# A hybrid attention/mLSTM encoder layer: the first stage loads x first, takes the modulation weights and the first projection by halves in an order written out by hand, and TensorE keeps the written order with its transposes among the products

## The chip, the cores and the metric

The kernel runs on one core of one Trainium2 chip. Its engines are TensorE (PE in the profile; its weight loads are PEld), VectorE (DVE), ScalarE (ACT), GpSimd (POOL) and SyncE (SP), which issues most of the DMAs. Each engine works through its own queue in order. The metric is the device time of one execution in microseconds (us), as the median of several runs; less is better.

## The reference: what is computed

One encoder layer on x of 2048 x 1024 in float32, then a last RMSNorm. Only the head of the layer matters here: the modulation vectors, the first norm, and the columns of the input projection that give the attention's values, the mLSTM's values and the gates.

```python
def hybrid_layer(x, c, w_mod, b_mod, g_norm1, w_in, ...):
    mod = jax.nn.silu(c) @ w_mod + b_mod                 # 6 x 1024
    shift1, scale1, gate1, shift2, scale2, gate2 = [m[:, None, :] for m in jnp.split(mod, N_MOD, axis=-1)]
    hmix = rms_norm(x, g_norm1) * (1.0 + scale1) + shift1
    proj = hmix @ w_in
    q_a, k_a, v_a, q_m, k_m, v_m, o_m, gates = jnp.split(proj, IN_SPLITS, axis=-1)
    ...                                                  # windowed attention, two mLSTM scans, w_out
    hff = rms_norm(x, g_norm2) * (1.0 + scale2) + shift2
    gte, up = jnp.split(hff @ w_ffn_in, 2, axis=-1)
    ff = (jax.nn.silu(gte) * up) @ w_ffn_out
    return x + gate2 * ff
```

## The kernel before

All products are made in three passes of a split float32: each operand is a rounded high part and the rest as a low part, and `mm3` (L55 to L58) issues high x high, high x low and low x high. So every operand needs a split, a copy (ACT or DVE) and a subtraction (DVE or POOL).

The first stage is the block under the pool `sw`. It does these things:

- **Modulation.** A modulation vector m is made by halves z of 512 columns. `load_mod` (L177) brings a half of `w_mod` in four tiles `wmod` of 512 KB. `mod_sum` (L190) sums the eight 128-row pieces, each scaled by a column of silu(c): on DVE into `macc` (L195, L197), or, for the first `n_pe` pieces, on TensorE (L201). TensorE turns the sum into columns (`modps`, L207 or L211), and `mod_bias` (L216) adds the bias. Only m = 1 (scale1) and m = 0 (shift1) are needed before the first norm is complete; m = 2 to 5 are made later, a half at a time, by `mod_row` (L320): four more 512 KB loads (L331), eight DVE operations (L335, L337), the split of `macc` (`macch`, `maccl`, L124 and L125), and two products with ones (`modrow`, L343 and L344).
- **Norm and transpose.** x comes in four blocks n of 512 rows, each four tiles `xt` of 512 KB. `normalised` (L146) squares on ACT (L151), takes the reciprocal root on DVE (`rsqrt`, 12 small operations), and scales the rows (L155 on ACT for block 0, L157 on DVE for the others). Then, for each of eight pieces k, `turned` (L159) makes four transposes on TensorE into one PSUM bank, "b" or "d" in turn, with one buffer each; ACT evicts the bank with scale and shift into `ntmp` (L164, two buffers); DVE splits it into `hT` (L172, L173).
- **Products.** `nat_mm` (L359) makes, for each of 16 tiles tt of 128 rows, 24 products of 272 columns into `pa` and 24 of 384 columns into `pv`. The weights are `wnl`/`wnh`, split from `wnr` in two halves by `split_nat` (L306). For tiles 0 to 2 the first half (k = 0 to 3) comes before the second.
- **Evictions and stores.** For each tile, ACT and DVE write `vs` (L404, L405, one buffer) and `gn` (L406), ACT writes `va` (L407, L408, two buffers), and SP stores `vst_d` (L412) and `vaug_d` (L413). A `mod_row` step follows from tile 4 on (`next(vecs)`, L411).

In this stage a scheduler sets the order of every engine's queue from its own estimates, taking the program's order as priority. From the second stage on, TensorE's order is the program's (`hand`), and shortly after also that of the other engines (`win`). SP's loads run in order too: an issue that waits for a free buffer holds up every issue behind it. Each DMA also waits for the one eight issues earlier.

The pool `s1` holds what only the norm needs; two of the four buffers that `mod_row` uses for m = 3 to 5 lie in its place (the pool `w`, opened after `xs.close()`), so their loads wait for the last transposes of block 3. The stage's end is the last `modrow` and the last tile's products; then the second stage begins with the transposes of the gates.

Of the kernel before, what the change touches and what calls it, by code (L numbers as in the profile page):

```python
# [21 lines left out]
P = 128  # L22
T = 2048
D = 1024
# [12 lines left out]
def hybrid_layer_kernel(  # L37
# [52 lines left out]
    O_C, O_G1, O_G2, O_CB, O_CW, O_BM, O_GA, O_GM = 0, 8, 16, 24, 32, 56, 104, 108  # L90
# [55 lines left out]
    def normalised(pl, xt, on_act=False):  # L146

        ssq = pl.tile([P, 4], F32, tag="ssq", name="ssq")
        for i in range(4):
            jk = pl.tile([P, D], BF16, tag="junk", name="junk", bufs=1)  # L150
            act.activation(jk, xt[i], AF.Square, accum_out=ssq[:, i:i + 1])  # L151
        r = rsqrt(pl, ssq, 4, D, "rs")
        for i in range(4):
            if on_act:
                act.activation(xt[i], xt[i], AF.Copy, scale=r[:, i:i + 1])  # L155
            else:
                dve.tensor_scalar(xt[i], xt[i], r[:, i:i + 1], None, MUL)  # L157
# [8 lines left out]
    def norm_block(pl, xt, gs, shift, dst):  # L166

        normalised(pl, xt, len(hT) == 1)
        for k in range(KT):
            t = pl.tile([P, 512], F32, tag="ntmp", name="ntmp", bufs=2)  # L170
            turned(t, xt, k, "bd"[k % 2], gs, shift)
            dve.tensor_copy(dst(0, k), t)  # L172
            dve.tensor_tensor(dst(1, k), t, dst(0, k).bitcast(F32), SUB)  # L173
            yield True
# [14 lines left out]
    def mod_sum(pl, m, z, ws_, n_pe):  # L189

        acc = pl.tile([P, 512], F32, tag="macc", name="macc")
        for k in range(n_pe, KT):
# [3 lines left out]
            else:  # L196
                dve.scalar_tensor_tensor(acc, w, sc_col[:, k:k + 1], acc, MUL, ADD)  # L197
        if n_pe:
# [9 lines left out]
        else:  # L208
            ps = bank("d", "modps")
            for k in range(4):  # L210
                pe.matmul(ps[:, k:k + 1], acc[:, k * P:(k + 1) * P], ones[:, 0:1], start=True, stop=True)  # L211
        mod_bias(m, z, ps)

# [28 lines left out]
    with tc.tile_pool(name="sw", bufs=2, side="right", reuse_waits="tile") as sw:  # L242
        c8 = s1.tile([8, P], F32, name="c8", bufs=1)
        rows = s1.tile([112, P], F32, name="rows", bufs=1)
        sp.dma_start(c8, c.rearrange("o (a b) -> (o a) b", b=P))
        def load_x(n):
# [8 lines left out]
        wm = {(1, 0): load_mod(1, 0)}  # L255
        xts = [load_x(0)]
        for src, o, n in ((c, O_C, 8), (g_norm1, O_G1, 8), (g_norm2, O_G2, 8), (conv_b, O_CB, 8),
                          (conv_w[0], O_CW, 24), (b_mod, O_BM, 48), (g_attn_out, O_GA, 4), (g_mlstm_out, O_GM, 4)):
            sp.dma_start(rows[o:o + n, :], src.rearrange("o (a b) -> (o a) b", b=P))
# [8 lines left out]
        ps = bank("a", "colps")  # L268
        pe.transpose(ps[:, :112], rows, ident[:112, :112])
        dve.tensor_copy(cols, ps[:, :112])  # L270
        dve.tensor_scalar(cvw, cols[:, O_CW:O_CW + 24].rearrange("p (j k) -> p j k", j=3), 0.5, None, MUL)
        dve.tensor_scalar(cvb, cols[:, O_CB:O_CB + KT], 0.5, None, MUL)
        dve.tensor_scalar(gml, cols[:, O_GM:O_GM + HM], 0.5, None, MUL)
# [6 lines left out]
        sp.dma_start(bg, b_gates[0].partition_broadcast(P))  # L280
# [6 lines left out]
        def start_mod(z):  # L287

            for m in (1, 0):
                if (m, z) not in wm:  # L290
                    wm[m, z] = load_mod(m, z)
            for m, n_pe in ((1, 0), (0, (0, 4)[z])):
                mod_sum(s1, m, z, wm[m, z], n_pe)
# [21 lines left out]
        def norm1(n, xt):  # L315
            hT.append(Kt(n, f"hT{n}"))
            return norm_block(s1, xt, gs1, mod[:, 0, :], hT[n])
# [41 lines left out]
        def nat_mm(n, i, pa, pv, ks):  # L359
            for o, cs in ((pa[:, :NA], slice(0, NA)), (pv[:, :NV], slice(NA, NA + NV))):  # L360
                for k in ks:
                    lh, ll = (hT[n](s, k, slice(i * P, (i + 1) * P)) for s in (0, 1))
                    mm3(o, lh, ll, wh[:, k, cs], wl[:, k, cs], k == 0, k == KT - 1)

        gn = cp.tile([P, 2, 2, HM, NT], F32, name="gn")
        bgv = bg.rearrange("p (d y h) -> p y d h", d=2, y=2)
        start_mod(0)
        wn = [load_nat(z) for z in range(2)]
        split_nat(0, wn[0])
        g0 = norm1(0, xts[0])  # L370
        deque(islice(g0, 4), 0)
        ops = {i: (bank("gga"[i], "pa"), bank("acc"[i], "pv")) for i in range(3)}
        for i in range(3):
            nat_mm(0, i, *ops[i], range(4))
        start_mod(1)
        split_nat(1, wn[1])
        deque(g0, 0)
        xts += [load_x(1), load_x(2)]
        for n in range(NB):
            if n + 1 < NB:  # L380
                deque(norm1(n + 1, xts[n + 1] if n < 2 else load_x(3)), 0)
            if n == 1:
                vecs = mod_row(2)
            if n + 2 == NB:
                deque(vecs, 0)
                wrow = deque(["w1h", "w1l", "wm0", "wm1"])
                xs.close()
                wp = ctx.enter_context(tc.tile_pool(name="w", bufs=1, side="left", reuse_waits="tile"))
                wslots.extend([(wp, 0), (wp, 1)])
                vecs = chain.from_iterable(mod_row(m) for m in range(3, 6))  # L390
            if n + 1 == NB:
                w_first = proj_cols(C_KM)
            for i in range(4):
                tt = 4 * n + i
                if n == 0 and i < 3:
                    pa, pv = ops[i]
                    nat_mm(n, i, pa, pv, range(4, KT))
                else:
                    pa, pv = bank("g", "pa"), bank("a", "pv")
                    nat_mm(n, i, pa, pv, range(KT))  # L400
# [9 lines left out]
                if n:  # L410
# [475 lines left out]
    hand, win = ExitStack(), ExitStack()  # L886
    steps = [gates(), w_out_ops()]
    due = [0, next(steps[1])]
    hand.enter_context(tc.manual_schedule(engines={mybir.EngineType.PE}))
# [931 lines left out]
```

## Time and profile before

| | us |
|---|---|
| median of 3 runs | 2373.31 |
| the runs | 2373.31, 2383.68, 2371.09 |
| the profiled execution's own time | 2375.25 |
| its span | 2373.5 |
| TensorE busy in the span | 2256.7 (95%) |
| TensorE busy from 0 to 50 us, summed from windows of 10 us | 26.0 |
| TensorE's waits for `macch` from 60 to 215 us | 13.7 |
| mean granted TensorE clock | 0.988 |

A row of the timeline gives start, duration, engine, line, operation, output and inputs, form and count, and in brackets the idle time ahead of it with what ended it. A row of windows gives for each engine its busy time and its instructions, then the granted clock, the share of the DMA engines and GB/s. What a wait is worth is read in its stage: an engine's idle time costs only where the next thing on TensorE hangs on it.

### The profile page before, as it was taken

What the parts mean: (1) busy time and instruction counts of PE and PEld (TensorE: products, weight loads), DVE (VectorE), ACT (ScalarE), POOL (GpSimd) and SP (SyncE); (2) the same over time, 40 slices, a digit from 0 to 9 for tenths busy, and PEclk for the clock granted to TensorE, in tenths of its full rate; (3) what the DMA queues carried; (4) which work ended last, traced back from release to release, by engine and by line L of the source; (5) the groups of instructions that cost most, each with busy time, mean ns of one, the idle gap of its engine ahead of it and who ended that gap; (6) DMA issues with size and microseconds to landing.
All of it is one profiled execution on the core that took longest, in us unless ns stands there. A gap on an engine that the chain in (4) does not pass through costs nothing.

```text
span 2373.5 us, 32635 instructions
## 1 busy us (share of the span) xinstructions
PE 2256.7 (95%) x10811; PEld 1870.8 (79%) x10811; DVE 1587.3 (67%) x2998; ACT 1074.2 (45%) x2205; POOL 1029.9 (43%) x876
## 2 busy tenths in 40 slices
PE   5988999999999989898999999999999999999998
PEld 4987777888788867787878878788888888888886
DVE  6777577667687877878555685755655536684684
ACT  4523555545487745435453443543434323233452
POOL 1004643334334434516555555465656545592020
PEclk9999999999999989999999999999999999999999
DMA  7575845577666566863343553533333373443452
GB/s 294 175 217 181 266 147 171 171 219 205 189 178 182 176 200 200 269 241 124 111 168 94 169 164 107 200 107 94 107 93 107 97 242 127 154 152 98 145 196 95
DMA packets 355517, 393.40 MB, mean 166 GB/s; under 512 B 21396, under 2 KB 253196, under 8 KB 355348
## 3 DMA queue, kind: packets, MB, share of 16 engines
q1 hardware_dynamic: 355348, 391.32, 51.9%
q8 instruction: 85, 1.39, 0.2%
q14 instruction: 84, 0.69, 0.1%
HBM read 272.06 MB, written 119.19 MB: 165 GB/s over the span
## 4 chain that ended last, share of the span: by engine, by line
PE 52%; DVE 3%; DMA 1%; issue 1%; ACT 1%; SPq 0%; POOL 0%; DVEq 0%; ACTq 0%; POOLq 0%
PE fp L56 11%; PE fp L57 11%; PE fp L58 11%; PE fo L58 6%; PE fo L57 6%; PE fo L56 6%; DVE S L1363 1%; PE ops L56 1%; PE ops L58 1%; PE ops L57 1%; DVE T L1323 0%; DVE A L1363 0%; PE trn L163 0%; DVE B L1323 0%; DMA hop_d<-n 0%
## 5 line engine op out<-in xcount | busy, mean ns | idle before, releaser
L424 PE MATMUL gps<-hT,whi 128*128 128x512 f32 x1088 | 398.2, 420 | 0.0
L56 PE MATMUL fo<-w,ah 128*128 128x512 f32 x616 | 241.7, 392 | 2.6 <-ACT ah L1605 2.6
L58 PE MATMUL fo<-w,al 128*128 128x512 f32 x616 | 241.8, 393 | 0.5 <-DVE al L1606 0.5
L57 PE MATMUL fo<-w,ah 128*128 128x512 f32 x616 | 241.5, 392 | 0.0
L424 PE MATMUL gps<-hT,wlo 128*128 128x512 f32 x544 | 228.3, 420 | 0.0
L56 PE MATMUL fp<-T,S 128*128 128x512 f32 x528 | 211.0, 400 | 12.2 <-ACT s L1508 6.4
L424 PEld LDWEIGHTS gps<-hT,whi 128*128 128x128 f32 x1088 | 202.6, 191 | 24.3 <-issue 0.2
L57 PE MATMUL fp<-T,S 128*128 128x512 f32 x528 | 209.1, 396 | 0.0
L58 PE MATMUL fp<-T,S 128*128 128x512 f32 x528 | 209.0, 396 | 0.0
L1606 DVE TENSOR_TENSOR al<-al,ah 128x1024 fp32r<-128x1024 f32 x77 | 112.7, 1468 | 130.2 <-ACT ah L1605 130.0
L1363 DVE TENSOR_TENSOR A<-graw,A 128x512 fp32r<-128x512 f32 x86 | 107.6, 1270 | 118.3 <-ACT A L1362 116.4
L1605 ACT ACTIVATE ah<-al 128x1024 fp32r<-128x1024 f32 x77 | 81.6, 1060 | 193.5 <-DMA al<-a_d 190.5
L56 PEld LDWEIGHTS fo<-w,ah 128*128 128x128 f32 x616 | 115.6, 188 | 29.2 <-ACT ah L1605 3.0
L58 PE MATMUL fp<-B,A 128*128 128x512 f32 x352 | 137.6, 391 | 0.0
L56 PE MATMUL fp<-B,A 128*128 128x512 f32 x352 | 137.6, 391 | 0.0
L57 PE MATMUL fp<-B,A 128*128 128x512 f32 x352 | 137.6, 391 | 0.0
L58 PEld LDWEIGHTS fo<-w,al 128*128 128x128 f32 x616 | 115.5, 188 | 27.2 <-DVE al L1606 1.0
L57 PEld LDWEIGHTS fo<-w,ah 128*128 128x128 f32 x616 | 115.5, 188 | 26.3
L56 PEld LDWEIGHTS fp<-T,S 128*128 128x128 f32 x528 | 100.7, 191 | 36.9 <-ACT u L1516 7.9
L716 POOL TENSOR_SCALAR ap<-ap,adn 128x384 f32<-128x384 f32 (+1 forms) x128 | 73.1, 590 | 127.1 <-DVE adn L714 57.4
L58 PEld LDWEIGHTS fp<-T,S 128*128 128x128 f32 x528 | 100.6, 191 | 22.6
L1363 DVE TENSOR_TENSOR S<-sf,S 128x512 fp32r<-128x512 f32 x86 | 87.3, 1017 | 45.8 <-ACT S L1362 45.8
(416 smaller groups left out, 6107.5 us busy)
## 6 DMA issues: line engine op xcount, KB each, us to landing
al<-a_d SPq DMA_DIRECT2D x77, 512.0 KB, 4.1
wmod<-in_w_mod_dram SPq DMA_DIRECT2D x48, 512.0 KB, 6.3
graw<-in_w_ffn_in_dram SPq DMA_DIRECT2D x43, 512.0 KB, 5.0
a_d<-ka SPq DMA_DIRECT2D x66, 256.0 KB, 2.4
bc<-bc_d SPq DMA_DIRECT2D x64, 256.0 KB, 3.8
hop_d<-n SPq DMA_DIRECT2D x56, 256.0 KB, 3.8
a_d<-u SPq DMA_DIRECT2D x55, 256.0 KB, 3.5
mqk<-qk_d SPq DMA_DIRECT2D x48, 256.0 KB, 4.4
```

Source lines behind the costliest of these rows:

```text
L56: pe.matmul(o, lh, rh, start=first, stop=False, skip_group_check=skip)
L57: pe.matmul(o, lh, rl, start=False, stop=False, skip_group_check=skip)
L58: pe.matmul(o, ll, rh, start=False, stop=last, skip_group_check=skip)
L424: pe.matmul(ps, w[i == 2][:, k, :], hT[n](i == 1, k), start=(k == 0 and i == 0), stop=(k == KT - 1 and i == 2))
L716: pool.tensor_scalar(self.p[g][:, :self.NK], self.p[g][:, :self.NK], dn[:, g:g + 1], 0.0, MUL, ADD)
L1363: dve.tensor_tensor(t[:, 1, :], f, t[:, 0, :].bitcast(F32), SUB)
L1605: act.activation(ah, al.bitcast(F32), AF.Copy)
L1606: dve.tensor_tensor(al, al.bitcast(F32), ah.bitcast(F32), SUB)
```

## The change

The first stage is rewritten in eight respects.

1. SP loads x's block 0 first, then scale1's and shift1's first halves, the projection weights' first half, scale1's second half, the weights' second half, shift1's second half, then blocks 1 and 2 of x. Before, scale1's first half came first, then x, nine small loads, and the rest.
2. The small vectors are split into two tiles; the part that is needed first (g_norm1 and b_mod) is issued by ACT, the rest by SP after block 2, and turned in the second block (`columns_of`).
3. Four of the eight pieces of scale1's first half are summed on TensorE instead of DVE; for shift1's second half this was so before.
4. From the start to the transposes of block 0's second half, all engines keep the program's order (`pre`, `hand`). The weights' second half is split after scale1's second sum, not among block 0's first pieces.
5. TensorE keeps the program's order for the whole stage. `nat_mm` yields after each k, and the table EVERY says after how many k a batch of four transposes of the next block is issued: block 1's in tile 3, block 2's two in each of tiles 4 to 7, block 3's all in tile 8. Before, block 1's stood among the second halves of tiles 0 to 3, and block 3's among the first 24 products of tile 8.
6. x's block 3 is loaded in the first round instead of the third.
7. `xs.close()` comes after tile 8's products, and tile 9 takes no `mod_row` step. The first `modrow` of m = 3 comes after tile 10, the last after tile 15.
8. `hand` is entered here instead of in the second stage.

The order of the second stage and of everything behind it is the same on all engines.

```diff
-    def norm_block(pl, xt, gs, shift, dst):
-
-        normalised(pl, xt, len(hT) == 1)
-        for k in range(KT):
-            t = pl.tile([P, 512], F32, tag="ntmp", name="ntmp", bufs=2)
...
+    def turned_split(pl, xt, k, gs, shift, dst):
+
+        t = pl.tile([P, 512], F32, tag="ntmp", name="ntmp", bufs=2)
+        turned(t, xt, k, "bd"[k % 2], gs, shift)
+        dve.tensor_copy(dst(0, k), t)
+        dve.tensor_tensor(dst(1, k), t, dst(0, k).bitcast(F32), SUB)
...
+        hand, pre = ExitStack(), ExitStack()
+        others = {getattr(mybir.EngineType, e) for e in ("DVE", "Activation", "Pool", "SP")}
+        hand.enter_context(tc.manual_schedule(engines={mybir.EngineType.PE}))
+        pre.enter_context(tc.manual_schedule(engines=others))
...
+        for src, o, n in ((g_norm1, O_G1, 8), (b_mod, O_BM, 48)):
+            act.dma_start(rows[0][o:o + n, :], src.rearrange("o (a b) -> (o a) b", b=P))
...
-        wm = {(1, 0): load_mod(1, 0)}
         xts = [load_x(0)]
...
+        wm = {(m, 0): load_mod(m, 0) for m in (1, 0)}
...
+        wn = [load_nat(0)]
+        wm[1, 1] = load_mod(1, 1)
+        wn.append(load_nat(1))
+        wm[0, 1] = load_mod(0, 1)
+        xts += [load_x(1), load_x(2)]
...
+        ms = {(m, z): mod_sum(s1, m, z, wm[m, z], 4 if m == 1 - z else 0) for z in range(2) for m in (1, 0)}
+        ssq = squares(s1, xts[0])
+        r = rsqrt(s1, ssq, 4, D, "rs")
+        next(ms[1, 0])
+        scaled(xts[0], r, True)
+        next(ms[0, 0])
...
+        scales(0)
+        split_nat(0, wn[0])
+        ops = {i: (bank("gga"[i], "pa"), bank("acc"[i], "pv")) for i in range(3)}
+        for k in range(4):
+            turned_split(s1, xts[0], k, gs1, mod[:, 0, :], hT[0])
+        for i in range(3):
+            deque(nat_mm(0, i, *ops[i], range(4)), 0)
+        next(ms[1, 1])
+        split_nat(1, wn[1])
...
+        scales(1)
+        for k in range(4, KT):
+            turned_split(s1, xts[0], k, gs1, mod[:, 0, :], hT[0])
+        pre.close()
...
+        EVERY = ((0, 0, 0, 2), (8, 8, 8, 8), (2, 0, 0, 0), (0, 0, 0, 0))
         for n in range(NB):
             if n + 1 < NB:
-                deque(norm1(n + 1, xts[n + 1] if n < 2 else load_x(3)), 0)
+                nrm = norm1(n + 1, xts[n + 1])
+                next(nrm)
+            if n == 0:
+                xts.append(load_x(3))
             if n == 1:
                 vecs = mod_row(2)
+                columns_of(1, N_A, N_B)
...
+                ev = EVERY[n][i]
+                for j, _ in enumerate(nat_mm(n, i, pa, pv, range(4 if tt < 3 else 0, KT))):
+                    if ev and j % ev == ev - 1:
+                        next(nrm, None)
+                if tt == 8:
+                    deque(nrm, 0)
+                    wrow = deque(["w1h", "w1l", "wm0", "wm1"])
+                    xs.close()
...
-                if n:
+                if tt != 9:
                     next(vecs, None)
```

Three places show how the queues change. The first is SP's at the start of the program; the names are the destination and the source in DRAM, and the counts stand behind. Before:

```order
L245 DMA c_102<-in_c_dram 8x128
L184 DMA wmod<-in_w_mod_dram 128x2x512 x4
L251 DMA xt<-in_x_dram 128x1024 x4
L259 DMA rows<-in_c_dram 8x128
L259 DMA rows<-in_g_norm_dram 8x128 x2
L259 DMA rows<-in_conv_b_dram 8x128
L259 DMA rows<-in_conv_w_dram 24x128
L259 DMA rows<-in_b_mod_dram 48x128
L259 DMA rows<-in_g_attn_out_dram 4x128
L259 DMA rows<-in_g_mlstm_out_dram 4x128
L280 DMA bg<-in_b_gates_dram 128x16
L184 DMA wmod<-in_w_mod_dram 128x2x512 x4
```

SP's first rows of the change:

```order
L253 DMA c_106<-in_c_dram 8x128
L261 DMA xt<-in_x_dram 128x1024 x4
L184 DMA wmod<-in_w_mod_dram 128x2x512 x8
L302 DMA wnr<-in_w_in_dram 128x4x128
L303 DMA wnr<-in_w_in_dram 128x4x16
```

The four tiles of x have moved ahead of the weights, and the nine small loads, `bg` among them, have left the place between two groups of 512 KB.

The second place is TensorE at the second halves of block 0. Before, with transposes (`trn`) taken as the scheduler saw fit:

```order
L211 MATMUL modps<-ones_r,macc 128x1 x4
L201 MATMUL modrow<-wmod,sc_col 1x512 x4
L163 MATMUL trn<-ident,xt 128x128 x4
L202 MATMUL modrow<-macc,ones_r 1x512
L207 MATMUL modps<-ones_r,mrow 128x1 x4
L163 MATMUL trn<-ident,xt 128x128 x8
L56 MATMUL pa<-wnh,hT_220 128x272
L57 MATMUL pa<-wnl,hT_220 128x272
L163 MATMUL trn<-ident,xt 128x128 x4
```

TensorE at the same place in the change:

```order
L213 MATMUL modps<-ones_r,macc 128x1 x4
L203 MATMUL modrow<-wmod,sc_col 1x512 x4
L204 MATMUL modrow<-macc,ones_r 1x512
L209 MATMUL modps<-ones_r,mrow 128x1 x4
L166 MATMUL trn<-ident,xt 128x128 x16
L56 MATMUL pa<-wnh,hT_211 128x272
L57 MATMUL pa<-wnl,hT_211 128x272
```

All sixteen transposes now stand behind the last modulation products and ahead of the first product.

The third place is DVE in the fifth half of the sums for m = 3 to 5, from one `maccl` (the low part that ends a half) to the next. Before:

```order
L337 SCALAR_TENSOR_TENSOR macc<-wmod,sc_col,macc 128x512
L357 TENSOR_TENSOR mod<-mod,cols 128x8
L337 SCALAR_TENSOR_TENSOR macc<-wmod,sc_col,macc 128x512
L415 SCALAR_TENSOR_TENSOR gs_88<-mod,cols 128x8
L405 TENSOR_TENSOR vs<-pa,vs 128x2x64
L337 SCALAR_TENSOR_TENSOR macc<-wmod,sc_col,macc 128x512
L406 TENSOR_TENSOR gn<-pa,bg 128x16
L337 SCALAR_TENSOR_TENSOR macc<-wmod,sc_col,macc 128x512 x3
L125 TENSOR_TENSOR maccl<-macc,macch 128x512
```

DVE in the same half of the change:

```order
L343 SCALAR_TENSOR_TENSOR macc<-wmod,sc_col,macc 128x512
L363 TENSOR_TENSOR mod<-mod,cols 128x8
L343 SCALAR_TENSOR_TENSOR macc<-wmod,sc_col,macc 128x512
L447 TENSOR_TENSOR vs<-pa,vs 128x2x64
L343 SCALAR_TENSOR_TENSOR macc<-wmod,sc_col,macc 128x512
L448 TENSOR_TENSOR gn<-pa,bg 128x16
L343 SCALAR_TENSOR_TENSOR macc<-wmod,sc_col,macc 128x512
L457 SCALAR_TENSOR_TENSOR gs_88<-mod,cols 128x8
L343 SCALAR_TENSOR_TENSOR macc<-wmod,sc_col,macc 128x512
L125 TENSOR_TENSOR maccl<-macc,macch 128x512
```

The eviction `vs` stands one operation later: four sums followed it, now three. In the second to sixth half the sums behind it were 3, 4, 4, 4, 4 and are 1, 2, 2, 3, 3.

91 lines of the change are left out of this document (42 added, 49 removed).

## The prediction

> **What bounds the kernel now.** The page comes first: TensorE is busy nearly all the time, so only its idle stretches can be won, and they are sought stage by stage in the windows.
>
> ```profile
> PE 2256.7 (95%) x10811; PEld 1870.8 (79%) x10811; DVE 1587.3 (67%) x2998; ACT 1074.2 (45%) x2205; POOL 1029.9 (43%) x876
> 0.00:10.00 10.00, 0.24 (x1) 0.18 (x1) 5.40 (x12) 1.49 (x2) 1.26 (x9) 1.00 0.79 281
> 10.00:20.00 10.00, 2.99 (x11) 2.33 (x11) 4.26 (x21) 7.03 (x11) 0.00 (x0) 1.00 0.72 237
> 20.00:30.00 10.00, 4.81 (x20) 3.79 (x19) 7.12 (x12) 4.28 (x7) 0.39 (x1) 1.00 1.09 383
> 77.00:116.00 39.00, 38.91 (x262) 37.97 (x262) 30.69 (x71) 15.42 (x31) 2.46 (x5) 1.00 0.55 178
> 130.00:200.00 70.00, 56.33 (x342) 53.61 (x341) 48.94 (x105) 15.13 (x35) 5.81 (x8) 0.98 0.69 209
> PE modrow L343 <- ACT macch L124: 13.7, 6, 3.8
> ```
>
> The first number behind the stretch is TensorE's busy time, with its instructions. It lacks 22 us of the first 30, nothing from 77 to 116, and 13.7 us of the last 70, all of it, by the list of waits (total, times, longest), at the six `modrow` products. So the first stage has a slow head and a slow tail with a full middle, in which 262 instructions take 39.0 us: 0.149 each, 7.2 for the 48 products of a tile and 4.8 for the 32 transposes of a block.
>
> The tail first, since its cause is not in the list. DVE, ACT, SP and TensorE in order of time:
>
> ```profile
> 138.99 0.63 ACT L124 ACTIVATE macch<-macc 128x512 fp32r<-128x512 f32 x1 [2.67 <-DVE macc L337]
> 149.21 0.46 SPq L412 DMA_DIRECT2D vst_d<-vs  x1
> 155.63 0.28 ACT L404 ACTIVATE vs<-pa 128x128 fp32r<-128x128 f32 x1 [4.24 <-DMA vst_d<-vs]
> 155.94 0.29 DVE L405 TENSOR_TENSOR vs<-pa,vs 128x128 fp32r<-128x128 f32 x1 [2.12 <-ACT vs L404]
> 156.93 2.33 DVE L337 SCALAR_TENSOR_TENSOR macc<-wmod,sc_col,macc 128x512 f32<-128x512 f32 x3
> 151.54 8.11 SPq L331 DMA_DIRECT2D wmod<-in_w_mod_dram  x4
> 159.71 0.46 SPq L412 DMA_DIRECT2D vst_d<-vs  x1
> 193.17 0.63 ACT L124 ACTIVATE macch<-macc 128x512 fp32r<-128x512 f32 x1 [3.06 <-DVE macc L337]
> 199.32 0.49 ACT L408 ACTIVATE va<-pv 128x384 f32<-128x384 f32 x1 [4.15 <-PE pv L58]
> ```
>
> This is a ring. The store of `vs` is issued at 149.21; the next `vs`, which has one buffer, starts only at 155.63, when that store has landed (6.4). DVE's part of it (155.94) stands in the middle of a half's eight sums. The rest of the sums ends at 159.26, which frees the fourth `wmod` buffer; SP's fourth load goes, and behind it in SP's queue the next store, at 159.71. One turn is 10.5 us, where a tile's products need 7.2, plus about 1.2 for `modrow`. From the first `macch` (138.99) to the sixth (193.17) the five turns take 54.2. The stage's last products end at about 199.2.
>
> **The head.** The rows that carry its terms, with two windows of DMA:
>
> ```profile
> 14.00:16.00 2.00, 0.39 (x1) 0.18 (x1) 0.54 (x5) 1.17 (x3) 0.00 (x0) 1.00 0.23 8
> 32.00:34.00 2.00, 2.00 (x9) 1.53 (x9) 1.97 (x3) 0.43 (x1) 1.02 (x1) 1.00 1.05 409
> 5.33 0.49 DVE L195 TENSOR_SCALAR macc<-wmod,sc_col 128x512 f32<-128x512 f32 x1 [1.85 <-DMA wmod<-in_w_mod_dram]
> 10.36 1.06 ACT L151 ACTIVATE junk<-xt 128x1024 bf16<-128x1024 f32 x1 [7.28 <-DMA xt<-in_x_dram]
> 15.39 0.17 DVE L99 TENSOR_SCALAR rsv<-ssq 128x4 f32<-128x4 f32 x1 [4.06 <-ACT junk L151]
> 17.56 4.27 ACT L155 ACTIVATE xt<-xt,rsy 128x1024 f32<-128x1024 f32 x4 [2.21 <-DVE rsy L106]
> L197 DVE SCALAR_TENSOR_TENSOR macc<-wmod,sc_col,macc x24: 750/752/753, 5.8 to 50.2; 128x512 f32<-128x512 f32 x24
> 26.16 1.83 PE L211 MATMUL modps<-ones_r,macc 128*128 128x1 f32 x8 [3.80 <-DVE macc L197]
> 28.23 0.78 ACT L164 ACTIVATE ntmp<-trn,mod,gs 128x512 f32<-128x512 f32 x1 [2.60 <-DVE mod L216]
> 44.97 0.33 PE L58 MATMUL pv<-wnh,hT 128*128 128x384 f32 x1
> 47.72 3.59 PE L201 MATMUL modrow<-wmod,sc_col 128*1 128x512 f32 x8
> 54.83 0.65 PE L163 MATMUL trn<-ident,xt 128*128 128x128 f32 x4 [0.26 <-DVE mod L216]
> 60.23 0.69 DVE L173 TENSOR_TENSOR hT<-ntmp,hT 128x512 fp32r<-128x512 f32 x1
> ```
>
> The small loads leave the DMA engines nearly empty around 15 (8 GB/s against 409): shift1's weights come late, and with them the scale and shift at 28.2.
>
> **The change, step by step.** I follow the new queues with these durations. All times are the profiled execution's.
>
> *To the first scale and shift.* At 409 GB/s a 512 KB tile takes 1.28. The first lands at 5.3, as `wmod` did; it is now x. The fourth lands at 9.2; its square (1.06 and 0.19 for the accumulator) ends at 10.4, the root takes 17.56 - 15.39 = 2.17, the scaling 4.27: x is ready at 16.9 (21.8 before). DVE sums four pieces of scale1 from the third tile's landing at 13.0 (0.49 + 3 x 0.75 = 2.74) and eight of shift1 (5.74): 21.5. `modps` takes 1.83, bias and scale 0.3: 23.7 against 28.2. **4.5 won.**
>
> *First halves.* Twelve tiles have landed by 5.3 + 11 x 1.28 = 19.4, and the weights' first 1.3 MB by 22.6. DVE makes its three parts of the split (2.5) and four times copy and subtraction (0.43 + 0.69), and ends at 23.7 + 2.5 + 4.5 = 30.7. TensorE then has 60 of the 72 products left, 8.9, in written order, so it cannot run ahead into other tiles as it did; a slow spell at the start (below) adds about 2. They end at about 42.0 instead of 45.3. **3.3 won.**
>
> *Second halves.* `modps` 1.0, `modrow` 3.59 and 1.0, the row's eviction and turning 1.7, two DVE operations 0.3: the transposes start at 49.6 (54.83), and DVE ends block 0 as far behind them as before, 6 us, at 55.6 (60.9). DVE's four sums of shift1 (2.74) lie beside the 3.59. **5.3 won.** But with every transpose first, and products in order, 60 of the 72 products come after 55.6, again with a slow start: 55.6 + 8.9 + 2 = 66.5. Tile 3 with its eight batches (7.2 + 4.8 = 12.0) ends at 78.5. Before, TensorE had at the row
>
> ```profile
> 76.32 0.65 PE L163 MATMUL trn<-ident,xt 128*128 128x128 f32 x4 [1.09 <-ACT ntmp L164]
> 34.85 0.52 PE L57 MATMUL pv<-wnl,hT 128*128 128x384 f32 x1
> 35.17 0.52 PE L58 MATMUL pv<-wnh,hT 128*128 128x384 f32 x1
> 43.20 0.34 PE L57 MATMUL pv<-wnl,hT 128*128 128x384 f32 x1
> 43.38 0.34 PE L58 MATMUL pv<-wnh,hT 128*128 128x384 f32 x1
> 69.11 0.66 PE L163 MATMUL trn<-ident,xt 128*128 128x128 f32 x4
> ```
>
> done all of block 1's transposes and, by its queue, 85 products; the other 35 up to the end of tile 3 take 5.2, to 82.2. **3.7 won.** The slow spell is seen in the `pv` rows: two such products start 0.32 apart in the first 4 us of work and 0.18 later, at a granted clock of 1.00 in both; so 4 us of it lose about 2.
>
> *Stalls of the written order.* `columns_of` takes bank "d" after block 1's last transposes and must wait for its eviction: 0.9. In tile 3 DVE has 8 x 1.12 for the splits, 2.1 for a root and 1.4 for `vs` and `gn`, 12.5 in TensorE's 12.0; with what is left from before it lags by about 1. The rows bound such a lag: 1.09 at 76.32 was the longest wait for an eviction, nothing the least. I take 1.9 in all, from a range of 0.9 to 8 (one wait of 1.09 at half of the sixteen batches of tiles 3 and 8). **1.8 left** at tile 8. Before, that tile started 24 products and 32 transposes (8.3) ahead of 124.4, at 116.1; now at 114.3.
>
> *Start of the tail.* The last transpose of block 3 (the row at 123.70) released `wmod`'s loads; now it ends behind 48 products, at 114.3 + 12.0 = 126.3.
>
> ```profile
> 123.70 0.66 PE L163 MATMUL trn<-ident,xt 128*128 128x128 f32 x4
> 124.84 2.28 SPq L331 DMA_DIRECT2D wmod<-in_w_mod_dram  x2
> 135.56 2.84 POOL L231 TENSOR_TENSOR wlo<-wraw,whi 128x1024 fp32r<-128x1024 f32 x1 [2.16 <-ACT whi L230]
> 132.27 6.68 DVE L337 SCALAR_TENSOR_TENSOR macc<-wmod,sc_col,macc 128x512 f32<-128x512 f32 x6
> ```
>
> From load to first `macch` it was 138.99 - 124.84 = 14.1. Six sums took 6.68 instead of 4.5 while POOL's split ran beside them; that stays. A wait for `vs` inside them goes (0.7). First `macch`: 126.3 + 13.4 = 139.7. **0.7 lost.** TensorE, though, has then done all of tile 10, 33 products more than at the old first `modrow`.
>
> *The ring.* It stays: one buffer of `vs`, the store behind the four loads. But DVE's `vs` moves back in each half: 3, 4, 4, 4, 4 sums stood behind it, now 1, 2, 2, 3, 3. Eight sums of 0.75 fall out of the ring, 6.0; the first turn gives 0.25 back, since DVE's own row of work is then as long. Five turns take 48.4 instead of 54.2: **5.8 won.** The sixth `macch` follows at 188.1 (193.17).
>
> *The end.* Before, the last `modrow` still had 18 products behind it, to 199.2. Now it is the last of the stage: 188.8 + 1.2 = 190.0. **9.2 won** in all; I say 9.5, since the head's terms are cut short where they meet the stalls. From there the orders are the same and TensorE is the bound, so I carry it to the end whole: 2375.25 - 9.5 = 2365.75 for the profiled execution. That one stood 1.94 above the median of 2373.31, so the median should be **2363.8**, 0.40% less.
>
> [...] The store in the ring costs 6.4 us by the rows above. [...]
>
> **The rivals.**
>
> *The ring lets go* (0.20). If a store lands soon after its issue, the list for `vs` has the value for that, TensorE sets the pace:
>
> ```profile
> DMA to landing us min/median/max: 1.7/1.7/1.7
> ```
>
> Then the six `modrow` products come 7.2 + 1.2 = 8.4 apart from the end of tile 10 (126.3 + 14.4 = 140.7), the last at 182.7, and the stage ends at 183.9: 15.3 won, or 17.2 with no stalls before. 2356 to 2358. For it: the store may meet the queue in another state. Against: it is still right behind a 512 KB load, as in the rows quoted.
>
> *The ring stays as long* (0.20): if another wait (the weights' landing, `pa`'s products) takes the place of the eight sums, only 9.5 - 5.8 = 3.7 is won, 2369.6.
>
> *Block 1 and block 3 in lockstep* (0.06), the other side. In tiles 3 and 8 a batch waits for a bank, the bank for ACT, ACT's `ntmp` for DVE. With two banks these overlap, but ACT and DVE have other work in their set places. If each of the 16 batches waited for the whole trip, 0.78 + 0.43 + 0.69 = 1.9, that is 30 us, so 21 lost: 2394. It decides once DVE needs more for a batch than the 1.5 us that six products and four transposes take (10 x 0.149); I count 12.5 / 8 = 1.56 in tile 3, near it.
>
> *Nothing arrives* (0.04): if the array fell to its slow pace beside the transposes of tiles 3 and 8, their 96 products (14.3) would take 0.32 / 0.18 as long, 11 more, and eat the gain: 2375. The four products after the batch at 69.11 start 0.18 to 0.26 apart, so hardly.
>
> **Chances and range.** The forecast has 0.50, with 2360 to 2368 as its own range, by 4 us for stalls and turns. A measurement of this kernel can tell about 0.5% from no change, 11.9 us, so the border is 2361.4. Faster: the ring's 0.20 and a third of the forecast, 0.37. Slower: 0.06. Within: 0.57. The range of 2355 to 2371.5 holds the forecast and its two neighbours and leaves out the last two rivals.
>
> **What would show it.** In the changed profile: `xt`'s first square at 5.3; the first `ntmp` at 24; DVE's last `hT` of block 0 at 55.6; the first load from `w_mod` for m = 3 into the `w` pool at 126; `macch` at 139.7 and 188, with turns of 8.5 to 10; the gates' transposes at 190. A store landing within 2 us, a wait over 2 us at a transpose in tiles 3 or 8, or a second stage that begins early and ends late would make it wrong.

## The result and the profile after

| | before | after |
|---|---|---|
| median, us | 2374.85 (6 runs) | 2360.3 (6 runs, 2357.82 to 2365.35) |
| ratio, with its 95% interval | | 0.9942 (0.9921 to 0.9962) |
| the profiled execution's own time, its span | 2375.25, 2373.5 | 2360.82, 2359.0 |
| first row of the gates on ACT, which ends the stage | 199.71 | 184.49 |

The change saves 14.6 us by the medians, 0.58% by the ratio, where the forecast had said 9.5 and 0.40%. The forecast's own range was 2360 to 2368, and 2360.3 stands at its edge; the interval lies on both sides of the 0.5% that was to tell faster from no change. All of it is won in the first stage: the gates come 15.2 us sooner, at 184.49 (below) instead of

```profile
199.71 0.28 ACT L760 ACTIVATE gates<-gps 128x128 f32<-128x128 f32 x1
```

and from there to the end it is 2173.8 before and 2174.5 after.

The windows of the changed profile, in the prediction's columns; the middle lies 4 to 5 us earlier than before, and the last window takes in the second stage's start:

```profile
0.00:10.00 10.00, 0.56 (x2) 0.36 (x2) 1.16 (x6) 4.94 (x8) 1.26 (x9) 1.00 0.70 233
10.00:20.00 10.00, 7.25 (x18) 1.80 (x18) 7.22 (x20) 6.00 (x7) 0.00 (x0) 1.00 1.05 404
72.00:112.00 40.00, 39.08 (x266) 38.17 (x265) 32.13 (x75) 15.05 (x32) 0.63 (x6) 1.00 0.56 179
130.00:200.00 70.00, 64.86 (x364) 58.32 (x363) 58.46 (x131) 19.32 (x40) 14.43 (x17) 0.95 0.74 238
```

The DMA engines are no longer partly idle from 10 to 20 (404 GB/s against 237). The middle lacks 0.9, one wait that is named below, and the last 70 us have 64.9 busy instead of 56.3. The waits of TensorE for `modrow`, once 13.7 us in one row, are now two small rows of the list (total, times, longest):

```profile
PE modrow L350 <- DVE maccl L125: 2.9, 5, 2.0
PE modrow L349 <- ACT macch L124: 2.3, 2, 1.2
```

The steps that the prediction dated, from the timeline:

```profile
5.00 1.06 ACT L151 ACTIVATE junk<-xt 128x1024 bf16<-128x1024 f32 x1 [1.79 <-DMA xt<-in_x_dram]
10.09 1.06 ACT L151 ACTIVATE junk<-xt 128x1024 bf16<-128x1024 f32 x1 [1.10 <-DMA xt<-in_x_dram]
13.44 4.26 ACT L158 ACTIVATE xt<-xt,rsy 128x1024 f32<-128x1024 f32 x4 [2.21 <-DVE rsy L106]
25.16 1.13 DVE L296 SCALAR_TENSOR_TENSOR gs<-mod,cols 128x4 f32<-128x4 f32 x1
26.39 1.45 ACT L167 ACTIVATE ntmp<-trn,mod,gs 128x512 f32<-128x512 f32 x2 [0.94 <-DVE gs L296]
32.48 0.39 PE L58 MATMUL pa<-wnh,hT 128*128 128x272 f32 x1 [0.21 <-DVE hT L174]
42.02 0.95 PE L213 MATMUL modps<-ones_r,macc 128*128 128x1 f32 x8
49.33 1.09 PE L166 MATMUL trn<-ident,xt 128*128 128x128 f32 x8 [0.26 <-DVE mod L220]
67.33 0.60 PE L166 MATMUL trn<-ident,xt 128*128 128x128 f32 x4
112.93 0.60 PE L166 MATMUL trn<-ident,xt 128*128 128x128 f32 x4
122.49 0.60 PE L166 MATMUL trn<-ident,xt 128*128 128x128 f32 x4
123.67 0.93 SPq L337 DMA_DIRECT2D wmod<-in_w_mod_dram  x2
136.02 0.63 ACT L124 ACTIVATE macch<-macc 128x512 fp32r<-128x512 f32 x1 [2.34 <-DVE macc L343]
180.11 0.61 ACT L124 ACTIVATE macch<-macc 128x512 fp32r<-128x512 f32 x1
184.49 0.28 ACT L802 ACTIVATE gates<-gps 128x128 f32<-128x128 f32 x1 [3.40 <-PE gps L799]
```

And one turn of the ring, in order of time:

```profile
144.66 0.46 SPq L454 DMA_DIRECT2D vst_d<-vs  x1
147.00 5.98 SPq L337 DMA_DIRECT2D wmod<-in_w_mod_dram  x4
150.53 0.28 ACT L446 ACTIVATE vs<-pa 128x128 fp32r<-128x128 f32 x1 [3.68 <-DMA vst_d<-vs]
150.84 0.29 DVE L447 TENSOR_TENSOR vs<-pa,vs 128x128 fp32r<-128x128 f32 x1
152.68 0.63 ACT L124 ACTIVATE macch<-macc 128x512 fp32r<-128x512 f32 x1 [0.43 <-DVE macc L343]
153.03 0.46 SPq L454 DMA_DIRECT2D vst_d<-vs  x1
```

The ring is still closed: store at 144.66, landed at 150.53 (5.9), next `vs`, two sums, next store at 153.03. But a turn is 8.4 us instead of 10.5, which is what TensorE itself needs for a tile and a `modrow`. The six `macch` start at 136.02, 144.31, 152.68, 160.96, 170.58 and 180.11: three turns of 8.3 to 8.4, then 9.6 and 9.5.

### The profile page after: what moved, and what is told of

The parts are those of the page before. It is cut to its first block, busy times and chain, and to the rows that moved or that the text cites. A ratio compares the mean times of both kernels' runs of the same rounds, so it can differ in the third digit from the quotient of the medians.

```text
span 2359.0 us, 32643 instructions
## 1 busy us (share of the span) xinstructions
PE 2262.5 (96%) x10822; PEld 1872.0 (79%) x10822; DVE 1578.8 (67%) x2995; ACT 1076.2 (46%) x2206; POOL 1032.2 (44%) x876
## 4 chain that ended last, share of the span: by engine, by line
PE 53%; DVE 3%; DMA 1%; issue 1%; ACT 1%; SPq 0%; POOL 0%; DVEq 0%; ACTq 0%; POOLq 0%
PE fp L56 11%; PE fp L57 11%; PE fp L58 11%; PE fo L58 6%; PE fo L56 6%; PE fo L57 6%; PE ops L56 1%; PE ops L58 1%; PE ops L57 1%; DVE S L1404 1%; DVE T L1364 0%; DVE A L1404 0%; PE trn L166 0%; DVE B L1364 0%; DMA x1t<-x_d 0%
## 5 line engine op out<-in xcount | busy, mean ns | idle before, releaser
L56 PEld LDWEIGHTS fo<-w,ah 128*128 128x128 f32 x616 | 116.0, 188 | 29.4 <-ACT ah L1646 3.2
L56 PEld LDWEIGHTS fp<-T,S 128*128 128x128 f32 x528 | 100.7, 191 | 37.3 <-ACT u L1557 8.3
L58 PEld LDWEIGHTS fp<-T,S 128*128 128x128 f32 x528 | 100.8, 191 | 22.6
L57 PEld LDWEIGHTS fp<-T,S 128*128 128x128 f32 x528 | 100.7, 191 | 21.6
```

The source lines that it names most:

```text
L56: pe.matmul(o, lh, rh, start=first, stop=False, skip_group_check=skip)
L57: pe.matmul(o, lh, rl, start=False, stop=False, skip_group_check=skip)
L58: pe.matmul(o, ll, rh, start=False, stop=last, skip_group_check=skip)
```

## The experiments

Each run was timed beside runs of the kernel before on the same chip. The ratios' intervals are some 0.002 to either side (4 us), so the steps are read from the traces, at two rows that every kernel has: ACT's `va` from `pv` of tile 9 and of tile 15, and the gates' first row. Two profiles of one kernel differ by 2.2 us at the gates (after and e9, e1 and e12); a smaller difference of one row is read only where the rows ahead of it show its cause. Part of the 2.2 has a cause that the traces show, a spell of 3.4 us at a granted clock of 0.50. In the changed kernel's profile it lies at 56.0 to 59.5, under products one behind the other; in e9's at 50.6 to 54.0, where TensorE waits for DVE in any case. Tile 3's first batch of transposes starts at 67.33 and at 65.96.

| kernel | tile 9's `va` | tile 15's `va` | six tiles | gates | ratio |
|---|---|---|---|---|---|
| before | 135.82 | 199.32 | 63.5 | 199.71 | 1 |
| e1, before + second vs | 135.19 | 186.71 | 51.5 | 187.10 | 0.9948 |
| e12, the same again | 137.59 | 188.90 | 51.3 | 189.28 | 0.9962 |
| e5, before, vst_d by POOL | 135.19 | 187.17 | 52.0 | 187.56 | 0.9972 |
| e3, before, x first | 139.00 | 200.71 | 61.7 | 201.10 | 1.0007 |
| after | 130.34 | 180.63 | 50.3 | 184.49 | 0.9942 |
| e9, after again | 129.00 | 178.43 | 49.4 | 182.29 | 0.9946 |
| e2, after + second vs | 129.62 | 178.75 | 49.1 | 182.62 | 0.9936 |
| e4, after, old tail | 136.85 | 193.56 | 56.7 | 193.94 | 0.9973 |
| e6, after, only TensorE set | 135.92 | 186.09 | 50.2 | 189.95 | 0.9986 |
| e7, after, n_pe 0 | 132.00 | 182.37 | 50.4 | 186.22 | 0.9966 |
| e8, after, batches in blocks | 134.75 | 180.82 | 46.1 | 183.78 | 0.9952 |
| e10, after, gap filled | 131.71 | 181.21 | 49.5 | 185.07 | 0.9954 |
| e11, after + second vs, n_pe 4 | 141.44 | 189.99 | 48.6 | 193.36 | 0.9972 |

So the change's 15.2 us are 5.5 up to tile 9, 13.2 in the six tiles behind it, and 3.5 given back between tile 15 and the gates (0.39 before, 3.86 after). The last two belong together: before, all six `modrow` steps stand in the six tiles; in the change the sixth stands behind tile 15.

### The ring: e1, e2, e12, e5

```diff
-                vs = sw.tile([P, KV, 2, HD], F32R, tag="vs", name="vs", bufs=1)
+                vs = sw.tile([P, KV, 2, HD], F32R, tag="vs", name="vs", bufs=2)
```

> The kernel before with a second vs buffer and nothing else. Theory of the ring: DVE's vs no longer waits for the store vst_d of the tile before, so the five turns from the first to the sixth macch (54.2 us before) fall to 42 to 48 us, the waits modrow for macch in the stage's tail (13.7 us) fall below 6, the stage ends at 187 to 193 instead of 199.2 and the span is 6 to 12 us shorter. Rival, that a turn is set by the landing of the weights of modulation or by DVE's sums themselves: turns stay at 10 to 11 us and the span within 2 us of before.

The kernel before with this one line: six tiles in 51.5 instead of 63.5, five turns in 44.7 instead of 54.2, gates 12.6 sooner, ratio 0.9948 (0.9931 to 0.9966). The ring's theory holds, at the top of its range, and its rival falls. The head is unchanged (135.19).

> The changed kernel with a second vs buffer. Theory of the ring: only the last two of the five turns (9.62 and 9.53 us) are still set by it, so they fall to 8.3 to 8.4 and the span gets 2 to 2.5 us shorter; the first three stay at 8.3. Rival, that the last two turns are long because the weights land late or DVE runs beside POOL: they stay at 9.5 and the span within 1 us of the changed kernel's.

Half as expected: the fourth turn falls from 9.62 to 8.28, but the fifth stays at 9.79, because ACT has another instruction in front:

```profile
177.27 1.06 ACT L234 ACTIVATE whi<-wraw 128x1024 fp32r<-128x1024 f32 x1 [1.86 <-DMA wraw<-in_w_in_dram]
178.23 0.61 ACT L124 ACTIVATE macch<-macc 128x512 fp32r<-128x512 f32 x1
```

The gates come 1.9 sooner, which two profiles of one kernel also differ by; the ratio is 0.9936 (0.9918 to 0.9954). That it beats the changed kernel isn't shown.

> The kernel before with a second vs buffer, again, beside the changed kernel on one chip. Theory that the ring is worth 12 us of the stage and the changed head 4 to 5 more with it, but the changed kernel keeps 2.4 of the ring's turns: this one stands 2 to 3 us behind the changed kernel (ratio 0.9945 to 0.9955) and its stage ends at 187. Rival, that all of the change's gain is the ring's: both ratios within 0.0005 of one another.

> The changed kernel itself, unchanged, beside the next three on the same chip: a ratio of 0.994 to before, 0.0055 to 0.0065 below 1, if the two comparisons are of one kind. If it comes out at 0.9965 or nearer to 1, the first comparison was lucky, and the head's share of the gain is not in the time.

Side by side: 0.9962 (0.9946 to 0.9978) for the one line, 0.9946 (0.9926 to 0.9967) for the change. The intervals lie over one another, so the times alone don't tell the two apart, and neither theory nor rival of e12 is shown by them; its stage ended at 189.28, where 187 was expected. The rows of the gates do tell them apart, at 187.10 and 189.28 against 184.49 and 182.29, with two profiles of each. The change's ratio came out at its second comparison as at its first. Most of its gain is the ring's, then: the one line has the gates 12.6 and 10.4 sooner, the change 15.2 and 17.4.

What closes the ring was tried another way, with one buffer:

```diff
-                sp.dma_start(vst_d[tt * P:(tt + 1) * P], vs.bitcast(F32))
+                pool.dma_start(vst_d[tt * P:(tt + 1) * P], vs.bitcast(F32))
```

> The kernel before, with its one vs buffer, but the store vst_d issued by POOL instead of SP. Theory that the ring is made of the store standing in one queue behind the loads of w_mod: the store lands 2 to 3 us after its issue instead of 6.4, vs is free when the next tile wants it, tile 9's va to tile 15's takes 50 to 55 us instead of 63.5, and the span is 8 to 12 us shorter, as with two buffers. Rival, that the store is slow because the loads take the DMA engines whatever queue it is in: it still lands 5 us or more after its issue, the six tiles take 60 us or more, and the span is less than 4 us shorter.

Both theories have a part. The six tiles took what the first said, the stores land as the second said. The view of the tensor `vst_d`, who waited for it and how long a store took (the list knows only some of the stores), in this kernel:

```profile
  ACT vs L404: 3.3, 3
DMA to landing us min/median/max: 2.0/3.9/5.3
```

Before, the first row read `ACT vs L404: 20.3, 5`. The stores still take up to 5.3 us, as the rival said, and yet the six tiles take 52.0: a store is issued 0.7 us behind DVE's `vs` (157.20 to 157.90) instead of 3.8 (155.94 to 159.71), since no load that waits for a buffer stands in front. So the place in the queue makes the ring longer than TensorE's own turn; a landing of 5.3 without it does not. (DVE's order came out another way here too, with five to eight sums behind each `vs`, so the queue is not all that differs.) The ratio, 0.9972 (0.9959 to 0.9984), is nearer to 1 than e1's, but its interval overlaps those of e1 and e12; a difference is not shown.

### The tail in its old order: e4

```diff
+            if n + 2 == NB:
+                deque(nrm, 0)
+                deque(vecs, 0)
...
-                if tt != 9:
+                if True:
```

> The changed kernel with the tail put back: all transposes of block 3, the closing of the x buffers and the generator of the m=3 to 5 vectors stand ahead of tile 8 again, and every tile takes a step of the vectors, tile 9 too. Theory that the tail's gain comes from how many DVE sums stand behind each vs (the ring): the head's 4.2 us stay (tile 8's first instruction at 112 to 113), the five turns go back to 50 to 54 us, and the span is 7 to 11 us longer than the changed kernel's. Rival, that the tail's gain comes from TensorE's set order alone: turns stay at 44 to 46 us and the span is within 3 us of the changed kernel's.

Behind the dots `xs.close()` and the vectors of m = 3 to 5 stand ahead of tile 8 again, and block 3's eight batches stand there with no products between them. That is not quite the old kernel, which had them among tile 8's products. The ratio is 0.9973 (0.9963 to 0.9983), and the gates come 9.5 later than in the changed kernel, 2.0 of it ahead of tile 8, where the two are the same program. So the size is as the first theory said, but its reason was wrong: the five turns take 46.1, close to its rival's 44 to 46, not 50 to 54. The scheduler put two, then three sums behind `vs` here, not four, and a turn took 9.0 to 9.4; that is 2.0. The largest part is another: the eight batches in front of tile 8 take 5.0 us more (its `va` comes 15.7 behind tile 7's, 10.75 in the changed kernel). That is a price of this edit, not of the old tail, since the kernel before needs 11.5 there (117.16 to 128.62). The list of waits has them; 3.0 of this row are six waits in front of tile 8:

```profile
PE trn L166 <- ACT ntmp L167: 3.7, 8, 0.8
```

The run shows something else besides. From 113.7 to 122.1 TensorE has nothing but transposes; the granted clock stays at 1.00, and the products behind them start at full pace, 0.125 apart:

```profile
121.73 0.66 PE L166 MATMUL trn<-ident,xt 128*128 128x128 f32 x4 [0.41 <-ACT ntmp L167]
122.35 0.29 PE L57 MATMUL pa<-wnl,hT 128*128 128x272 f32 x1
122.47 0.29 PE L58 MATMUL pa<-wnh,hT 128*128 128x272 f32 x1
```

### Batches in blocks: e8

```diff
-        EVERY = ((0, 0, 0, 2), (8, 8, 8, 8), (2, 0, 0, 0), (0, 0, 0, 0))
+        EVERY = ((0, 0, 0, 1), (1, 0, 0, 0), (1, 0, 0, 0), (0, 0, 0, 0))
```

> The changed kernel with the eight batches of transposes of each next block put one behind each of the first eight groups of products of the block's tile 3, 0 and 0 (EVERY of 1), instead of two groups apart or, for block 2, two batches in each tile. Theory that a batch needs its ntmp buffer back from DVE, about 1.1 us a batch (eight in a row with no products between took 5.0 us more than tile 8's): three products and a batch take 1.05 to 1.15, so TensorE waits 0 to 0.2 us at a batch and the span is 1 to 4 us longer. Rival, that every batch off its cover costs a full lockstep of 1.9 us: 24 of them, of which most wait, make it 15 us or more longer. Rival, that spreading them is worth nothing: within 1 us.

Up to tile 9 it costs 4.4, just above the first theory's 1 to 4; at the gates nothing is left of it (0.7 sooner, ratio 0.9952, 0.9935 to 0.9969). The tail has paid it back, with all five turns at 8.4 to 8.5. SP and DVE in this kernel:

```profile
140.52 0.28 DVE L447 TENSOR_TENSOR vs<-pa,vs 128x128 fp32r<-128x128 f32 x1
140.83 0.34 SPq L454 DMA_DIRECT2D vst_d<-vs  x1
141.27 1.97 SPq L337 DMA_DIRECT2D wmod<-in_w_mod_dram  x2
143.93 1.95 SPq L337 DMA_DIRECT2D wmod<-in_w_mod_dram  x2
148.22 0.28 DVE L447 TENSOR_TENSOR vs<-pa,vs 128x128 fp32r<-128x128 f32 x1
148.50 4.68 DVE L343 SCALAR_TENSOR_TENSOR macc<-wmod,sc_col,macc 128x512 f32<-128x512 f32 x6
148.53 0.34 SPq L454 DMA_DIRECT2D vst_d<-vs  x1
```

The scheduler's order for DVE and SP came out another way in this kernel; what in the edit turned it isn't shown: the store goes 0.3 us behind `vs`, two loads behind it, two more later, and six sums or more stand behind `vs` without harm. This corrects the prediction's picture: the number of sums behind `vs` is not a price by itself; it counts where the store stands behind a load that waits for those sums.

### The head: e3, e6, e7, e10, e11

```diff
-        wm = {(1, 0): load_mod(1, 0)}
         xts = [load_x(0)]
+        wm = {(m, 0): load_mod(m, 0) for m in (1, 0)}
...
-            sp.dma_start(rows[o:o + n, :], src.rearrange("o (a b) -> (o a) b", b=P))
+            act.dma_start(rows[o:o + n, :], src.rearrange("o (a b) -> (o a) b", b=P))
```

> The kernel before with x loaded first, then both first halves of the w_mod columns, and the parameter rows and bg issued by ACT instead of SP; no order is set. Theory that the head's gain is the order of the loads: scale and shift are ready 2 to 4.5 us earlier than at 28.2, tile 8 starts at 112 to 114 instead of 116.1, the tail from there to the stage's end keeps its 83 us, and the span is 2 to 4 us shorter. Rival, that the set order of the engines is what makes the head faster: tile 8 starts within 1 us of 116.1 and the span is within 1.5 us of before.

The span is as the rival said, ratio 1.0007 (0.9995 to 1.0019), but the head is worse than either: 3.2 us later at tile 9. DVE and ACT:

```profile
14.90 0.16 DVE L99 TENSOR_SCALAR rsv<-ssq 128x4 f32<-128x4 f32 x1
15.02 0.75 DVE L197 SCALAR_TENSOR_TENSOR macc<-wmod,sc_col,macc 128x512 f32<-128x512 f32 x1
21.10 4.27 ACT L155 ACTIVATE xt<-xt,rsy 128x1024 f32<-128x1024 f32 x4 [6.75 <-DVE rsy L106]
30.71 0.78 ACT L164 ACTIVATE ntmp<-trn,mod,gs 128x512 f32<-128x512 f32 x1 [4.77 <-DVE mod L216]
```

The first square starts at 7.01 (5.00 in the change), since ACT has its nine DMA issues in front, and the last at 13.2 (14.2 before), after a wait of 2.69 for x's fourth tile. Then the scheduler puts sums between the steps of the root, which takes 6.2 instead of 2.2, and scaling starts at 21.1, later than the 17.6 of before.

```diff
-        pre.enter_context(tc.manual_schedule(engines=others))
```

> The changed kernel with TensorE's set order alone; DVE, ACT, POOL and SP are ordered by the scheduler again in the first stage. Theory that the head's gain needs the set order: DVE's sums get in between the steps of rsqrt again (6 us instead of 2.2), x is scaled 2 to 4 us later than at 17.7, scale and shift come at 27 to 29 instead of 25.2, and the span is 2 to 4 us longer than the changed kernel's. Rival, that the order of the loads and the halves on TensorE are enough: scale and shift within 1 us of 25.2 and the span within 1 us.

The loss is right and larger (5.6 at tile 9, ratio 0.9986, 0.9973 to 0.9999), the place wrong: the root stays at 2.2 here, and scale and shift come only 1.5 later. What DVE does then costs more:

```profile
29.52 3.44 DVE L314 TENSOR_TENSOR wnl<-wnr,wnh 128x512 fp32r<-128x512 f32 x2
38.09 3.46 DVE L198 SCALAR_TENSOR_TENSOR macc<-wmod,sc_col,macc 128x512 f32<-128x512 f32 x2
49.09 0.95 PE L213 MATMUL modps<-ones_r,macc 128*128 128x1 f32 x8
```

Parts of the split and sums of the second half stand among the four pieces of x, beside POOL, and the first halves end at 49.1 instead of 42.0. DVE's last piece ends 5.7 later (38.2 against 32.4); the other 1.3 fit the products that run here at a granted clock of 0.50, which lasts to 41.2. So the head's whole gain needs the set order of the four engines, and by these rows it is DVE's: e6 has all the loads in the new order, e3 x ahead of the weights, and neither has any of it at tile 9.

```diff
-        ms = {(m, z): mod_sum(s1, m, z, wm[m, z], 4 if m == 1 - z else 0) for z in range(2) for m in (1, 0)}
+        ms = {(m, z): mod_sum(s1, m, z, wm[m, z], 4 if (m, z) == (0, 1) else 0) for z in range(2) for m in (1, 0)}
```

> The changed kernel with the sums of the first half of scale all on DVE (n_pe 0 instead of 4 for m=1, z=0). Theory that DVE's sums set when scale and shift are ready: four sums of 0.75 come back, 3 us, so scale and shift come at 28 instead of 25.2 and the span is 2 to 3 us longer. Rival, that the halves of w_in and their split set the first products: the span is within 1 us of the changed kernel's.

Scale and shift come at 29.4, 4.1 later, and the first halves end at 45.3, 3.3 later. At tile 9 and at the gates 1.7 is left of it; the ratio is 0.9966 (0.9953 to 0.9979). But the changed kernel's granted clock falls to 0.51 and 0.64 from 56 to 60, and this run's stays at 1.00. Tile 3's first batch in the changed kernel, in e9 and here:

```profile
67.33 0.60 PE L166 MATMUL trn<-ident,xt 128*128 128x128 f32 x4
65.96 0.60 PE L166 MATMUL trn<-ident,xt 128*128 128x128 f32 x4
69.06 0.60 PE L166 MATMUL trn<-ident,xt 128*128 128x128 f32 x4
```

From the second halves' first transposes to this row it is 18.0, 16.5 and 16.5. Beside e9, whose slow spell cost nothing there, e7 is 3.1 later here, 3.0 at tile 9 and 3.9 at the gates. So by these rows the theory holds: DVE's sums set the head, and some 3 us of them reach the tail.

```diff
+        pw = bank("c", "warm")
+        for i in range(44):
+            pe.matmul(pw[:, :P], ones_r, ones_r, start=i == 0, stop=i == 43)
         next(ms[0, 0])
```

> The changed kernel with 44 matrix instructions more whose result nobody reads, set on TensorE into its gap between 20.0 and 23.2 us, where the sums of shift are waited for; after that gap the granted clock was 0.50 from 22 to 29 us. Theory that the gap sets the clock back and that this costs time: with the gap filled the clock stays at 1.00 up to 50 us, the first half's products end 1 to 2 us sooner than at 42.0, and the stage ends 1 to 2 us sooner. Rival, that TensorE waits for DVE's hT there anyway: the clock is 1.00, and the stage's end moves by less than 0.7 us. Rival, that short instructions do not hold the clock: 0.50 again in that stretch.

The clock does what the theory says up to 50 us, and the time what the first rival says. From 22 to 29 us, in the changed kernel and then in this one:

```profile
22.00:29.00 7.00, 5.45 (x25) 5.05 (x26) 5.04 (x10) 4.27 (x7) 2.53 (x2) 0.52 1.05 402
```

```profile
22.00:29.00 7.00, 6.55 (x56) 5.92 (x54) 3.83 (x10) 4.22 (x7) 2.50 (x2) 1.00 1.05 401
```

The clock is 1.00 instead of 0.52, and the first halves end at 42.09 instead of 42.02: TensorE waits there for DVE's pieces, 1.06 apart, up to 32.5. One part is not tested: the 44 instructions ran to about 25, so that `modps` waited for them (25.09, 23.18 in the changed kernel), and what the slow clock costs at `modps` itself (1.86 there, 1.00 here) stays open. The gates come 0.6 later, ratio 0.9954 (0.9937 to 0.9971), but behind 50 us this run has two slow spells where the changed kernel has one, so only the row at 42 can be compared.

```diff
+        ms = {(m, z): mod_sum(s1, m, z, wm[m, z], 0 if (m, z) == (1, 1) else 4) for z in range(2) for m in (1, 0)}
```

> The changed kernel with a second vs buffer, and with four of the eight sums of shift's first half on TensorE as well (n_pe 4 for m=0, z=0). Theory that DVE's sums set scale and shift, and that the ring is gone with the second buffer: scale and shift come 2 to 3 us sooner than at 25.2 and the gap on TensorE closes; the stage ends at 180 to 182 instead of 184.5, and the ratio to before is 0.992 to 0.993, below the changed kernel's. Rival, that w_in's first half (its last part lands at about 23) and its split then set the products: scale and shift come sooner but tile 8 starts within 0.7 us of the changed kernel's, and the stage ends at 182.6 as with the second buffer alone.

Wrong on both sides: scale and shift come at 30.8, 5.6 later, and the gates 8.9 later (10.7 later than e2's, which has the second buffer too), ratio 0.9972 (0.996 to 0.9984).

```profile
22.71 5.29 PE L203 MATMUL modrow<-wmod,sc_col 128*1 128x512 f32 x8 [2.46 <-DVE mod L220]
30.76 1.25 DVE L296 SCALAR_TENSOR_TENSOR gs<-mod,cols 128x4 f32<-128x4 f32 x1
```

DVE is done with both sums at 22.5, but TensorE's second row must wait for the bias of the first, then takes 5.3, and its row is turned behind that. Halving DVE's sums helps only while TensorE's half lies beside them.

## Why the prediction was right, and where it was not

Its direction and its two sources hold: a few us in the head, more in the ring. The size does not: 15.2 us at the gates, where the sum had 9.2 (it was then rounded up to 9.5, and no row stands for the 0.3). Point by point:

- **x first.** The first square comes at 5.00 (5.3 said), x is ready at 17.7 (16.9): x's last two tiles landed late, the waits of 0.40 and 1.10. Scale and shift were said for 23.7 and the first `ntmp` for 24; it comes at 26.39. DVE's sums begin at 14.3, not 13.0, and `gs`, once 0.16, takes 1.13 beside POOL. 1.8 won, not 4.5.
- **First halves** end at 42.02 (42.0, though its terms add to 41.6), by luck: the start is 2.4 late, and the slow spell of 2 us costs nothing behind the first pieces, since TensorE waits for DVE there anyway, as e10 shows. The transposes of the second halves at 49.33 (49.6) and tile 3 at 66.6 (66.5) are right, the latter with a slow spell of 3.4 us under its products, which e9 and e7 don't have there.
- **Stalls and transposes** were sized too high. The wait of 0.9 at `columns_of` is there, DVE's lag of 1.0 is not, and four transposes among products take 0.44 (tile 3's batches are 1.20 apart, with six products of 0.126 between), 3.5 for a block, not 4.8: 0.149 was the mean of products and transposes. Tile 8 starts at 112.2 (114.3), its last batch at 122.49, the loads at 123.67 (126.3), the first `macch` at 136.02 (139.7). These 3.7 us are missing in the sum.
- **The ring** is what bounded the tail: e1 and e12 take it away with one line, and the six tiles take 12.0 and 12.2 less. The step that was too small is its sum, 48.4 for five turns where 44.1 were measured. It took the store's landing as fixed at 6.4, but with two sums behind `vs` it was 5.7 to 5.9; and its last turn kept the 4.38 us of three sums beside POOL's split, which now runs behind them.
- **The end.** That split lies beside `maccl` instead (2.42 us, 0.69 before), so the gates come 4.4 behind the last `macch`, where 1.9 was said: 2.5 given back. 3.7 + 4.3 - 2.5 is 5.5, the distance from 190.0 to 184.5. It was carried to the end, as said: of 15.2 at the gates 14.5 are left in the span. In both kernels a spell at a granted clock of 0.50 goes with the last waits for `macch` and `maccl`. Before, it ends at 197.3, ahead of the gates; in the change it lasts from 182.3 to 189.2 and slows the second stage's first products, 0.43 apart instead of 0.23, which the row of the gates doesn't count.

Of the rivals, "the ring lets go" said 15.3 and 15.2 came, but not by its condition: the stores in the turns took 5.4 to 6.3 us to land. That its number came is luck, then. Three turns are as short as TensorE allows all the same. "Stays as long" falls with e1. The lockstep shows only where no products lie between the batches, in e4 (5.0 for eight); in tiles 3 and 8 of the change TensorE doesn't wait at all. And TensorE kept its pace beside the transposes, at a granted clock of 1.00 from 72 to 112, and in e4 behind 8 us of nothing but transposes, so "nothing arrives" falls too.

Open is which of the changed kernel, e2 and e8 is fastest: their intervals lie over one another.

## What to carry to other kernels

Where an engine that issues DMAs works in order, look for a store that stands behind loads which wait for buffers, and for what waits for that store: a ring of this kind shows in no single wait, and a second buffer, or another queue for the store, opens it. Loading the first input first won nothing here until the engines that use it also kept the order. Where a scheduler sets the queues, an edit in one stretch can turn the order in the next: e8 lost 4.4 us ahead of the tail and got them back there, so each stretch has to be read by itself. And a difference of 1 or 2 us between two profiles can be the place where a slow spell fell, as in e7 and e9.

## What the runs showed of the hardware

- A gap of 3.2 us on TensorE (20.0 to 23.2) went with a granted clock of 0.50 from 21.9 to 28.7; with 44 short instructions in the gap it was 1.00 there and up to 50 (e10). What decides when such a spell starts was not shown: one and the same kernel has its spells at 21.9 and 56.0 in one profile and at 23.3 and 50.6 in the other (e9). What a spell costs hangs on what it meets: 1.5 us under products one behind the other (18.0 us in the changed kernel from the second halves' first transposes to tile 3, 16.5 in e9), nothing where TensorE waits (the first halves end at 42.02 with a spell and at 42.09 without one, in e10). But the column is no proof of pace ahead of the first fall: in e7 a gap of 5.9 us (21.5 to 27.4) leaves 1.00 in it, and the first products behind it start 0.23 us apart, not 0.126.
- 36 transposes without a product between them (113.7 to 122.1 in e4) left the granted clock at 1.00 and the products behind them at full pace.
- Some DVE instructions beside POOL's split took a multiple of their time: the subtraction `maccl` 2.42 instead of 0.69, the small `gs` 1.13 instead of 0.16 (0.15 in e7 and e10, where POOL does nothing at that moment).
